# Opening of a two-layer decoder trunk: one modulation accumulator, scaling and rounding on ScalarE, products by parts

## The chip, the cores and the metric

The kernel runs on one core of a Trainium2 chip. The metric is the device time of one execution in microseconds (us). The engines of a core work side by side, each through its own list of instructions in order: TensorE (PE, matmuls; PEld is its weight load), VectorE (DVE), ScalarE (ACT), GpSimd (POOL) and SyncE (SP), which here starts the loads from memory. Times inside a profile are counted from the start of the profiled execution's span.

## The reference

Two layers, each of a SwiGLU half step, a token mixer and another SwiGLU half step. Every sub-layer normalizes its input and modulates it with shift and scale, which come from the condition c through mod_w:

```python
c_act = jax.nn.silu(c)
for i in range(DEPTH):
    mod = (c_act @ mod_w[i] + mod_b[i]).reshape(B, N_SUBLAYERS, 3, D)
    shift, scale, gate = mod[:, :, 0], mod[:, :, 1], mod[:, :, 2]
    h = modulate(rms_norm(x, norm_g[i, 0]), shift[:, 0], scale[:, 0])
    x = x + MACARON_WEIGHT * gate[:, 0, None, :] * swiglu(h, ffn_w_gate[i, 0], ffn_w_up[i, 0], ffn_w_down[i, 0])
    ...
```

with modulate(h, shift, scale) = h * (1 + scale) + shift and swiglu(h) = (silu(h @ w_gate) * (h @ w_up)) @ w_down. x has 256 tokens of 1024 channels, the SwiGLU has 2816 inner columns, all in float32. The change lies in the first sub-layer of the first layer: its rms_norm, its shift and scale, and the first 1536 columns of h @ w_gate and h @ w_up.

## The kernel before

A float32 product is made of three faster ones. Each operand is split into a rounded high part and the low rest: ScalarE copies the raw tile into the high part (wh, hTh), VectorE subtracts that from the raw values (wl, hTl), and TensorE adds wh x hTh, wh x hTl and wl x hTh in one PSUM bank (mm_blocks, L389 to L391). A matmul there takes 128 weight columns and 256 tokens.

open_trunk (L671 to L845) is the opening. VectorE, ScalarE, GpSimd, TensorE and SP run it in the order in which the code issues it. It first loads c and x, gets the row statistics (square on ScalarE, rms_scale on VectorE and GpSimd), scales x by them (u, L708, VectorE), transposes it on TensorE and copies it to xT (L712, ScalarE). Shift and scale of the 1024 channels are not ready then. They are made in four groups of two k-tiles (a k-tile is 128 channels): reduce multiplies eight 128-row slices of mod_w (tiles oraw, 128x512) with c and adds them up on VectorE (L756 opens an accumulator, L758 adds to it) into two accumulators, cacc0 and cacc1; modulate sums these over the partitions with products against a column of ones on TensorE (L770), makes scale and shift columns of the result (sb, three short VectorE steps), then h from xT (hk, L780, VectorE), its high part (hTh, L783, ScalarE) and its low part (hTl, L786, VectorE).

With a group's two k-tiles of h, TensorE can do six pieces of 12 matmuls: for each k-tile the first 512 gate columns, the first 512 up columns, and the next 512 gate columns. A group needs three weight tiles (raw, 128x1024): (0,k) holds gate and up columns of one k-tile, (1,k) the next gate columns of both. split makes wh on ScalarE (L743) and wl on VectorE (L744). There are four raw buffers and eight for pairs of oraw slices.

The table OPEN_HOLD sets how many pieces of a group are held back behind the next group's column sum (3, 2, 2), OPEN_SPLIT how many weight tiles are split ahead of the sb steps (2, 2, 2, 1), OPEN_HEAD and OPEN_MEAN where the next group's accumulations stand. After the last group the general weight stream starts (Weights, L215 for its wl, L206 for its wh), with up columns of the same SwiGLU. The two casts idr<-ident (L1026) belong to tables for the later attention and only stand in VectorE's list here; they wait for a memset of idr on GpSimd (L1024).

## Time and profile before

| | us |
|---|---|
| median of 3 runs | 1229.28 |
| lowest, highest run | 1228.28, 1230.29 |
| profiled execution, its own time | 1230.24 |
| its span, first to last instruction | 1228.5 |
| TensorE busy | 1202.4 |
| VectorE busy | 936.6 |
| ScalarE busy | 657.4 |

The profile is one execution. Busy time of TensorE counts the time in which a matmul is under way. A share over the whole span says little of the opening, the first 62 us of it; that stretch is read from its own rows.

### The profile page before, as it was taken

The numbers are of one execution on the slowest core, as the hardware profiler recorded it, in microseconds if no ns is written. First come the engines' busy times: TensorE is split into PE (matmuls) and PEld (weight loads), VectorE is DVE, ScalarE is ACT, GpSimd is POOL, SyncE is SP. The second block draws the span as 40 slices with busy tenths as digits, with TensorE's granted clock in tenths as the row PEclk, the third lists the DMA queues.
The fourth block names the chain that finished last, engine by engine and source line by source line (L and its number), as shares of the span: only waits on it lengthen the run. The fifth ranks groups of instructions, "written<-read, shape, count | busy, mean of one in ns | idle before, by whom it ended". The sixth has DMA issues, their size and how long they took to land.

```text
span 1228.5 us, 21017 instructions
## 1 busy us (share of the span) xinstructions
PE 1202.4 (98%) x8130; PEld 1085.5 (88%) x8130; DVE 936.6 (76%) x1318; ACT 657.4 (54%) x1002; POOL 101.9 (8%) x130
## 2 busy tenths in 40 slices
PE   6999999999999999999999999999999999999998
PEld 5999988878779999889999887888888787999987
DVE  7878777998788887579978659978686877765653
ACT  4446444676654554444554435677575665544540
POOL 1000000222100000000000003131131200000000
PEclk9999999999999999999999999999999999999999
DMA  9879885695739988638888647656545552866461
GB/s 334 277 269 327 304 317 182 199 306 201 272 99 341 330 275 310 206 111 292 305 277 325 206 154 235 210 181 211 175 154 182 197 173 86 289 203 217 168 213 42
DMA packets 152069, 281.21 MB, mean 229 GB/s; under 512 B 13424, under 2 KB 79504, under 8 KB 151968
## 3 DMA queue, kind: packets, MB, share of 16 engines
q1 hardware_dynamic: 151968, 279.85, 68.4%
q8 instruction: 64, 1.05, 0.3%
q14 instruction: 37, 0.30, 0.1%
HBM read 277.71 MB, written 2.10 MB: 228 GB/s over the span
## 4 chain that ended last, share of the span: by engine, by line
PE 76%; DVE 9%; DMA 5%; issue 4%; POOL 2%; ACT 2%; SPq 0%; POOLq 0%; DVEq 0%; ACTq 0%
PE block_bank L389 13%; PE block_bank L391 13%; PE block_bank L390 13%; PE bank L394 11%; PE bank L395 11%; PE bank L396 11%; DMA mraw<-in_mod_w_dram 3%; DVE wl L215 2%; POOL hrs L860 2%; DVE acc L296 1%; DVE lo L924 1%; PE obank L949 1%; DMA raw<-in_dil_w_in_dram 1%; DMA raw<-in_fox_w_in_dram 1%; ACT wh L206 1%
## 5 line engine op out<-in xcount | busy, mean ns | idle before, releaser
L215 DVE TENSOR_TENSOR wl<-raw,wh 128x1024 fp32r<-128x1024 f32 (+1 forms) x360 | 434.9, 1216 | 160.1 <-ACT wh L206 156.8
L206 ACT CAST wh<-raw 128x1024 fp32r<-128x1024 f32 (+1 forms) x360 | 374.5, 1046 | 299.2 <-PE bank L396 107.2
L389 PE MATMUL block_bank<-hTh,wh 128*128 128x256 f32 x1312 | 371.6, 283 | 2.0 <-ACT hTh L783 2.0
L391 PE MATMUL block_bank<-hTh,wl 128*128 128x256 f32 x1312 | 371.4, 283 | 0.0
L390 PE MATMUL block_bank<-hTl,wh 128*128 128x256 f32 x1312 | 370.7, 283 | 0.0
L389 PEld LDWEIGHTS block_bank<-hTh,wh 128*128 128x128 f32 x1312 | 248.5, 189 | 2.5 <-ACT hTh L783 2.1
L390 PEld LDWEIGHTS block_bank<-hTl,wh 128*128 128x128 f32 x1312 | 248.2, 189 | 0.5 <-DVE hTl L786 0.2
L391 PEld LDWEIGHTS block_bank<-hTh,wl 128*128 128x128 f32 x1312 | 248.0, 189 | 0.0
L394 PE MATMUL bank<-wh,hTh 128*128 128x512 f32 (+2 forms) x496 | 192.0, 387 | 0.8 <-DVE nm L924 0.8
L396 PE MATMUL bank<-wh,hTl 128*128 128x512 f32 (+2 forms) x496 | 181.6, 366 | 0.0
L395 PE MATMUL bank<-wl,hTh 128*128 128x512 f32 (+2 forms) x496 | 181.0, 365 | 0.0
L296 DVE SCALAR_TENSOR_TENSOR acc<-mraw,ccols,acc 128x1024 f32<-128x1024 f32 x112 | 143.4, 1281 | 29.8 <-DMA mraw<-in_mod_w_dram 29.3
L395 PE MATMUL bank<-wl,aTh 128*128 128x512 f32 (+1 forms) x420 | 146.4, 349 | 0.0
L394 PE MATMUL bank<-wh,aTh 128*128 128x512 f32 (+1 forms) x420 | 146.1, 348 | 0.0
L396 PE MATMUL bank<-wh,aTl 128*128 128x512 f32 (+1 forms) x420 | 145.7, 347 | 0.0
L396 PEld LDWEIGHTS bank<-wh,hTl 128*128 128x128 f32 x496 | 93.2, 188 | 16.5 <-DVE hTl L471 0.5
L394 PEld LDWEIGHTS bank<-wh,hTh 128*128 128x128 f32 x496 | 93.6, 189 | 14.0 <-DVE nm L924 1.2
L395 PEld LDWEIGHTS bank<-wl,hTh 128*128 128x128 f32 x496 | 93.7, 189 | 12.3
L394 PEld LDWEIGHTS bank<-wh,aTh 128*128 128x128 f32 x420 | 79.5, 189 | 10.8
L396 PEld LDWEIGHTS bank<-wh,aTl 128*128 128x128 f32 x420 | 79.3, 189 | 10.5
L395 PEld LDWEIGHTS bank<-wl,aTh 128*128 128x128 f32 x420 | 79.5, 189 | 10.1
L926 ACT ACTIVATE lo<-lo,nm 128x128 f32<-128x128 f32 (+1 forms) x64 | 37.8, 591 | 64.8 <-DVE nm L924 64.7
(225 smaller groups left out, 1280.9 us busy)
## 6 DMA issues: line engine op xcount, KB each, us to landing
mraw<-in_mod_w_dram SPq DMA_DIRECT2D x128, 512.0 KB, 5.2
raw<-in_ffn_w_down_dram SPq DMA_DIRECT2D x88, 512.0 KB, 4.1
raw<-in_ffn_w_gate_dram SPq DMA_DIRECT2D x76, 512.0 KB, 4.4
raw<-in_ffn_w_up_dram SPq DMA_DIRECT2D x76, 512.0 KB, 4.6
raw<-in_dil_w_in_dram SPq DMA_DIRECT2D x128, 256.0 KB, 4.2
raw<-in_fox_w_in_dram SPq DMA_DIRECT2D x36, 256.0 KB, 4.8
oraw<-in_mod_w_dram SPq DMA_DIRECT2D x32, 256.0 KB, 6.3
raw<-in_ffn_w_gate_dram SPq DMA_DIRECT2D x24, 256.0 KB, 6.0
```

The costliest lines, as they stand in the source:

```text
L206: act.copy(wh, self.raws[self.hi])
L215: dve.tensor_sub(wl, self.raws[self.lo], wh.bitcast(F32))
L296: dve.scalar_tensor_tensor(acc, raw, ccol[:, k:k + 1], self.bias_tile if k == 0 else acc, op0=OP.mult, op1=OP.add)
L389: pe.matmul(out_i, wh[:, blk], hTh[:, :, k, :], start=first and i % 2 == 0, stop=False)
L390: pe.matmul(out_i, wh[:, blk], hTl[:, :, k, :], start=False, stop=False)
L391: pe.matmul(out_i, wl[:, blk], hTh[:, :, k, :], start=False, stop=last and i % 2 == 1)
L394: pe.matmul(o, ah, wh, start=first, stop=False)
L395: pe.matmul(o, ah, wl, start=False, stop=False)
L396: pe.matmul(o, al, wh, start=False, stop=last)
L860: nc.gpsimd.tensor_tensor(rs, ms, mhalf, op=OP.pow)
L924: dve.tensor_tensor_reduce(out=lo[:, 0:n], in0=lg[:, 0:n], in1=m, scale=-1.0, scalar=BIG, op0=OP.add, op1=OP.min, accum_out=nm)
L926: act.activation(lo[:, 0:n], lo[:, 0:n], AF.Exp, bias=nm, scale=-1.0, accum_out=sums[:, t, i:i + 1])
```

## The change

Each group has one accumulator, opened by VectorE in group 0 and by ScalarE in the others, so its column sum has half as many products. Scaling of x moves to ScalarE, all accumulations of group 0 stand after it, and the columns of norm_g and mod_b are transposed between the two token tiles. hTh is made by ScalarE straight from xT, with scale and bias as per-partition operands; hk by VectorE in group 0 and by ScalarE afterwards. split is parted into split_hi and split_lo. The products of a piece run by parts (mm_parts): four with wh and hTh, four with wh and hTl, four with wl and hTh. One piece is held back in each group. Loads are issued in the same order.

```diff
-OPEN_HEAD = 4
-OPEN_SPLIT = (2, 2, 2, 1)
-OPEN_MEAN = (1, 2, 2)
-OPEN_HOLD = (3, 2, 2)
+OPEN_HOLD = 1
...
+    def mm_parts(o, k, wh, wl, first, last):
+
+        for w, h in ((wh, hTh), (wh, hTl), (wl, hTh)):
+            for i in range(4):
+                blk = slice(i * P, (i + 1) * P)
+                pe.matmul(o[i // 2][:, i % 2], w[:, blk], h[:, :, k, :], start=first and w is wh and h is hTh and
+                          i % 2 == 0, stop=last and w is wl and i % 2 == 1)
...
-        def normalize(t):
-            ss = main.tile([P, 2], F32, tag="ss", bufs=4, name="ss")
-            for h in range(2):
-                square(t, h, slice(h * 512, (h + 1) * 512), ss)
-            rs = rms_scale(ss)
...
-            def half(h):
-                xn = main.tile([P, 512], F32, tag="u", bufs=3, name="u")
-                dve.tensor_scalar(xn, x[t][:, h * 512:(h + 1) * 512], rs, None, op0=OP.mult)
-                tp = bank4()
-                for k in range(4):
-                    pe.transpose(tp[:, k, :], xn[:, k * P:(k + 1) * P], ident)
-                act.copy(xT[:, t, h * 4:(h + 1) * 4, :], tp)
-
-            return [lambda: half(0), lambda: half(1)]
+        def normalize():
+
...
+            held = []
+            for t in range(NT):
+                for h in range(2):
+                    xn = main.tile([P, 512], F32, tag="u", bufs=3, name="u")
+                    act.activation(xn, x[t][:, h * 512:(h + 1) * 512], AF.Copy, scale=rs[t])
+                    tp = bank4()
+                    for k in range(4):
+                        pe.transpose(tp[:, k, :], xn[:, k * P:(k + 1) * P], ident)
+                    held.append((xT[:, t, h * 4:(h + 1) * 4, :], tp))
+                    if len(held) == 3:
+                        act.copy(*held.pop(0))
+                if t == 0:
+                    columns(gb8, 3, gbcol)
+            for dst, tp in held:
+                act.copy(dst, tp)
...
-        def split(key):
+        def split_hi(key):
             raw = ws[key]
             wh = wp.tile([P, 2, 512], F32R, tag="wh", name="wh")
             wl = wp.tile([P, 2, 512], F32R, tag="wl", name="wl")
             act.copy(wh, raw)
-            dve.tensor_sub(wl, raw, wh.bitcast(F32))
-            ws[key] = wh, wl
+            ws[key] = wh, wl, raw
             uses[key] = 2
             weights.live += 1
 
+        def split_lo(key):
+            wh, wl, raw = ws[key]
+            dve.tensor_sub(wl, raw, wh.bitcast(F32))
+
...
-        def reduce(q, rows, extra=()):
+        def reduce(q, k):
             n = groups[q][1]
-            for k in rows:
-                if k < 2:
-                    accs[q, k] = pool.tile([P, 2, 2 * P], F32, tag=f"cacc{k}", bufs=2, name=f"cacc{k}")[:, :, 0:n * P]
-                    dve.tensor_scalar(accs[q, k], raws[q, k], ccol[:, k:k + 1], None, op0=OP.mult)
+            if k == 0:
+                accs[q] = pool.tile([P, 2, 2 * P], F32, tag="cacc", bufs=2, name="cacc")[:, :, 0:n * P]
+                if q:
+                    act.activation(accs[q], raws[q, k], AF.Copy, scale=ccol[:, k:k + 1])
                 else:
-                    dve.scalar_tensor_tensor(accs[q, k % 2], raws[q, k], ccol[:, k:k + 1], accs[q, k % 2],
-                                                   op0=OP.mult, op1=OP.add)
-                if extra:
-                    extra.pop(0)()
-
-        def modulate(q, between, meanwhile):
+                    dve.tensor_scalar(accs[q], raws[q, k], ccol[:, k:k + 1], None, op0=OP.mult)
+            else:
+                dve.scalar_tensor_tensor(accs[q], raws[q, k], ccol[:, k:k + 1], accs[q], op0=OP.mult, op1=OP.add)
+
+        def modulate(q):
+
             k0, n = groups[q]
             cp = bank()
-            terms = [(accs[q, i], ones.bitcast(F32)[:, 0:1]) for i in range(2)]
             for j in range(2):
                 for i in range(n):
-                    for m, (a, c) in enumerate(terms):
-                        pe.matmul(cp[:, n * j + i:n * j + i + 1], a[:, j, i * P:(i + 1) * P], c,
-                                         start=m == 0, stop=m == len(terms) - 1)
-            between()
+                    pe.matmul(cp[:, n * j + i:n * j + i + 1], accs[q][:, j, i * P:(i + 1) * P],
+                              ones.bitcast(F32)[:, 0:1], start=True, stop=True)
...
-            hk = pool.tile([P, NT, 2, P], F32, tag="hk", bufs=2, name="hk")
+            hk = pool.tile([P, 2, NT, P], F32, tag="hk", bufs=2, name="hk")
             for i in range(n):
-                dve.tensor_scalar(hk[:, :, i, :], xT[:, :, k0 + i], sb[:, 1, i:i + 1], sb[:, 0, i:i + 1],
-                                        op0=OP.mult, op1=OP.add)
-            for t in range(NT):
-                act.copy(hTh[:, t, ks, :], hk[:, t, 0:n])
-            meanwhile()
-            for t in range(NT):
-                dve.tensor_sub(hTl[:, t, ks, :], hk[:, t, 0:n], hTh[:, t, ks, :].bitcast(F32))
+                act.activation(hTh[:, :, k0 + i, :], xT[:, :, k0 + i], AF.Identity, scale=sb[:, 1, i:i + 1],
+                               bias=sb[:, 0, i:i + 1])
+                if q:
+                    act.activation(hk[:, i], xT[:, :, k0 + i], AF.Identity, scale=sb[:, 1, i:i + 1],
+                                   bias=sb[:, 0, i:i + 1])
+                else:
+                    dve.tensor_scalar(hk[:, i], xT[:, :, k0 + i], sb[:, 1, i:i + 1], sb[:, 0, i:i + 1],
+                                      op0=OP.mult, op1=OP.add)
+                yield lambda i=i: dve.tensor_sub(hTl[:, :, k0 + i, :], hk[:, i], hTh[:, :, k0 + i, :].bitcast(F32))
...
             k = wk + (i if w else 0)
-            mm_blocks(outs[o], k, wh[:, i], wl[:, i], k == 0, k == KT - 1)
+            mm_parts(outs[o], k, wh[:, i], wl[:, i], k == 0, k == KT - 1)
             uses[w, wk] -= 1
...
         load_mod(0, range(KT))
         load_weights(0)
-        halves = normalize(0) + normalize(1)
-        reduce(0, range(KT), halves)
-        columns(gb8, 3, gbcol)
+        normalize()
+        for k in range(KT):
+            reduce(0, k)
         backlog = []
         for q in range(nq):
-            todo = keys(q)
+            units, more = keys(q), range(0)
             if q:
                 load_weights(q)
-                reduce(q, rest)
-
-            def between():
-                for _ in range(OPEN_SPLIT[q]):
-                    if todo:
-                        split(todo.pop(0))
-
-            def meanwhile():
-                if q + 1 < nq:
-                    load_mod(q + 1, range(KT))
-                    reduce(q + 1, range(OPEN_MEAN[q]))
-
-            modulate(q, between, meanwhile)
-            while todo:
-                split(todo.pop(0))
+            split_hi(units[0])
+            lows = modulate(q)
+            next(lows)()
+            split_lo(units[0])
+            for low in lows:
+                low()
+            for u in units[1:]:
+                split_hi(u)
             if q + 1 < nq:
-                reduce(q + 1, range(OPEN_MEAN[q], OPEN_HEAD))
-            else:
+                load_mod(q + 1, range(KT))
+                reduce(q + 1, 0)
+                more = range(1, KT)
+            early = 2 if q else 0
+            for i, u in enumerate(units[1:]):
+                for k in more[early * i:early * (i + 1)]:
+                    reduce(q + 1, k)
+                split_lo(u)
+            for k in more[early * (len(units) - 1):]:
+                reduce(q + 1, k)
+            if q + 1 == nq:
                 weights.start()
             for piece in backlog:
                 products(piece)
             todo = pieces(q)
-            cut = len(todo) if q == nq - 1 else max(0, len(todo) - OPEN_HOLD[q])
+            cut = len(todo) if q == nq - 1 else len(todo) - OPEN_HOLD
             for piece in todo[:cut]:
                 products(piece)
```

**Place 1, VectorE, group 0's accumulations.** In the listings, msq and u are statistics and scaled x, cacc0, cacc1 and cacc the accumulators, oraw slices of mod_w. Before:

```order
L407 SCALAR_TENSOR_TENSOR msq_149<-ss_144 128x1
L756 TENSOR_SCALAR cacc0_153<-oraw_115,ccols_87 128x512
L708 TENSOR_SCALAR u_155<-x0_83,rs_142 128x512
L756 TENSOR_SCALAR cacc1_163<-oraw_115,ccols_87 128x512
L708 TENSOR_SCALAR u_165<-x0_83,rs_142 128x512
L758 SCALAR_TENSOR_TENSOR cacc0_153<-oraw_118,ccols_87,cacc0_153 128x512
```

VectorE at the same place in the change:

```order
L412 SCALAR_TENSOR_TENSOR msq_149<-ss_144 128x1
L1042 CAST idr_965<-ident_74 16x16 x2
L693 COPY gbcol_88<-bank_167 128x24
L774 TENSOR_SCALAR cacc_188<-oraw_115,ccols_87 128x512
L776 SCALAR_TENSOR_TENSOR cacc_188<-oraw_115,ccols_87,cacc_188 128x512
L776 SCALAR_TENSOR_TENSOR cacc_188<-oraw_118,ccols_87,cacc_188 128x512 x2
```

The scaling of x has gone, and the idr casts and the gbcol copy, which stood behind the eight accumulations, stand ahead of the first.

**Place 2, VectorE and ScalarE between the column sums of groups 1 and 2.** wl_341 is the low part of the tile of group 1's second k-tile before, wl_338 the same in the change; wl_452 and wl_456 are tiles of group 2, wl_315 and wl_335 tiles (0,2) and (1,2) of group 1; the accumulations are group 2's. VectorE before, from the end of hk on:

```order
L756 TENSOR_SCALAR cacc0_334<-oraw_322,ccols_87 128x512
L756 TENSOR_SCALAR cacc1_336<-oraw_322,ccols_87 128x512
L786 TENSOR_TENSOR hTl_86<-hk_317,hTh_85 128x256 x2
L744 TENSOR_TENSOR wl_341<-raw_289,wh_340 128x1024
L758 SCALAR_TENSOR_TENSOR cacc0_334<-oraw_325,ccols_87,cacc0_334 128x512
L758 SCALAR_TENSOR_TENSOR cacc1_336<-oraw_325,ccols_87,cacc1_336 128x512
L758 SCALAR_TENSOR_TENSOR cacc0_334<-oraw_328,ccols_87,cacc0_334 128x512
L758 SCALAR_TENSOR_TENSOR cacc1_336<-oraw_328,ccols_87,cacc1_336 128x512
L758 SCALAR_TENSOR_TENSOR cacc0_334<-oraw_331,ccols_87,cacc0_334 128x512
L758 SCALAR_TENSOR_TENSOR cacc1_336<-oraw_331,ccols_87,cacc1_336 128x512
L744 TENSOR_TENSOR wl_452<-raw_430,wh_451 128x1024
L744 TENSOR_TENSOR wl_456<-raw_433,wh_455 128x1024
```

VectorE in the change, from the end of the sb steps on:

```order
L801 TENSOR_TENSOR hTl_86<-hk_326,hTh_85 128x2x128
L763 TENSOR_TENSOR wl_315<-raw_306,wh_314 128x1024
L801 TENSOR_TENSOR hTl_86<-hk_326,hTh_85 128x2x128
L776 SCALAR_TENSOR_TENSOR cacc_352<-oraw_340,ccols_87,cacc_352 128x512
L776 SCALAR_TENSOR_TENSOR cacc_352<-oraw_343,ccols_87,cacc_352 128x512
L763 TENSOR_TENSOR wl_335<-raw_309,wh_334 128x1024
L776 SCALAR_TENSOR_TENSOR cacc_352<-oraw_343,ccols_87,cacc_352 128x512
L776 SCALAR_TENSOR_TENSOR cacc_352<-oraw_346,ccols_87,cacc_352 128x512
L763 TENSOR_TENSOR wl_338<-raw_311,wh_337 128x1024
L776 SCALAR_TENSOR_TENSOR cacc_352<-oraw_346,ccols_87,cacc_352 128x512
L776 SCALAR_TENSOR_TENSOR cacc_352<-oraw_349,ccols_87,cacc_352 128x512 x2
```

ScalarE at this place before, from the last split ahead of the column sum to the first of the next group:

```order
L743 CAST wh_309<-raw_287 128x1024
L783 CAST hTh_85<-hk_317 128x256 x2
L743 CAST wh_340<-raw_289 128x1024
L743 CAST wh_451<-raw_430 128x1024
L743 CAST wh_455<-raw_433 128x1024
```

ScalarE in the change, over the same stretch:

```order
L793 ACTIVATE hTh_85<-xT_108,sb_322 128x2x128
L796 ACTIVATE hk_326<-xT_108,sb_322 128x256
L793 ACTIVATE hTh_85<-xT_108,sb_322 128x2x128
L796 ACTIVATE hk_326<-xT_108,sb_322 128x256
L756 CAST wh_334<-raw_309 128x1024
L756 CAST wh_337<-raw_311 128x1024
L772 ACTIVATE cacc_352<-oraw_340,ccols_87 128x512
```

The low part of the second k-tile's tile stood right behind hTl and ahead of six accumulations; now four accumulations and another tile's low part stand ahead of it, and the first of these accumulations reads what ScalarE writes last in its listing.

**Place 3, TensorE, from the second to the third piece of group 1.** Before, in pieces of the same weight tiles:

```order
L389 MATMUL block_bank_112<-hTh_85,wh_305 128x256
L390 MATMUL block_bank_112<-hTl_86,wh_305 128x256
L391 MATMUL block_bank_112<-hTh_85,wl_306 128x256
L389 MATMUL block_bank_109<-hTh_85,wh_340 128x256
L390 MATMUL block_bank_109<-hTl_86,wh_340 128x256
L391 MATMUL block_bank_109<-hTh_85,wl_341 128x256
```

TensorE in the change:

```order
L395 MATMUL block_bank_112<-hTh_85,wl_315 128x256 x2
L395 MATMUL block_bank_109<-hTh_85,wh_337 128x256 x2
L395 MATMUL block_bank_110<-hTh_85,wh_337 128x256 x2
L395 MATMUL block_bank_109<-hTl_86,wh_337 128x256 x2
L395 MATMUL block_bank_110<-hTl_86,wh_337 128x256 x2
L395 MATMUL block_bank_109<-hTh_85,wl_338 128x256 x2
L395 MATMUL block_bank_110<-hTh_85,wl_338 128x256 x2
```

The products with the low part wl_338 now come ninth to twelfth in the piece; before, the first of them was the third product.

## Rows read from the trace of the kernel before

**Rows 1.** The page: busy us, share of the span, instructions, by engine.

```profile
PE 1202.4 (98%) x8130; PEld 1085.5 (88%) x8130; DVE 936.6 (76%) x1318; ACT 657.4 (54%) x1002; POOL 101.9 (8%) x130
```

**Rows 2.** Busy time by stretch; after the colon its length, then each engine.

```profile
core 0: us, PE busy (x) PEld busy (x) DVE busy (x) ACT busy (x) POOL busy (x), PEclk, DMA share, GB/s
...
19.85:61.80 41.95, 41.95 (x338) 41.75 (x339) 37.12 (x63) 18.78 (x25) 0.00 (x0) 1.00 0.89 299
61.80:230.00 168.20, 168.19 (x1182) 157.07 (x1181) 134.89 (x142) 84.52 (x105) 5.47 (x9) 1.00 0.78 266
```

**Rows 3.** TensorE in order of time: start, duration, engine, line, operation, tiles.

```profile
19.85 0.58 PE L389 MATMUL block_bank<-hTh,wh 128*128 128x256 f32 x1 [2.03 <-ACT hTh L783]
...
24.35 0.33 PE L390 MATMUL block_bank<-hTl,wh 128*128 128x256 f32 x1
...
26.41 1.84 PE L770 MATMUL bank<-ones,cacc 128*128 128x1 f32 x16
28.11 0.36 PE L389 MATMUL block_bank<-hTh,wh 128*128 128x256 f32 x1
...
38.15 1.84 PE L770 MATMUL bank<-ones,cacc 128*128 128x1 f32 x16
...
48.47 1.84 PE L770 MATMUL bank<-ones,cacc 128*128 128x1 f32 x16
...
61.54 0.28 PE L391 MATMUL block_bank<-hTh,wl 128*128 128x256 f32 x1
```

**Rows 4.** VectorE in order of time, in the opening.

```profile
7.68 0.49 DVE L756 TENSOR_SCALAR cacc<-oraw,ccols 128x512 f32<-128x512 f32 x1
...
11.89 2.73 DVE L758 SCALAR_TENSOR_TENSOR cacc<-oraw,ccols,cacc 128x512 f32<-128x512 f32 x4
...
14.63 0.33 DVE L1026 CAST idr<-ident 16x16 fp32r<-16x16 f32 x2
...
17.86 0.16 DVE L775 SCALAR_TENSOR_TENSOR sb<-bank,gbcol 128x2 f32<-128x2 f32 x1 [0.32 <-PE bank L770]
...
18.32 0.73 DVE L780 TENSOR_SCALAR hk<-xT,sb 128x256 f32<-128x256 f32 x2
...
36.61 2.35 DVE L744 TENSOR_TENSOR wl<-raw,wh 128x1024 fp32r<-128x1024 f32 x2
```

**Rows 5.** GpSimd in order of time, the memset of idr.

```profile
10.58 0.38 POOL L1024 MEMSET idr<- 128x16 f32 x1
```

**Rows 6.** VectorE in order of time after the opening, a single accumulator.

```profile
71.37 1.28 DVE L296 SCALAR_TENSOR_TENSOR acc<-mraw,ccols,bias 128x1024 f32<-128x1024 f32 x1
72.68 1.28 DVE L296 SCALAR_TENSOR_TENSOR acc<-mraw,ccols,acc 128x1024 f32<-128x1024 f32 x1
```

**Rows 7.** VectorE by line, 0 to 62 us: busy us, mean ns, idle before.

```profile
L758 DVE SCALAR_TENSOR_TENSOR cacc<-oraw,ccols,cacc 128x512 f32<-128x512 f32 x24 | 16.5, 749 | 0.0
L786 DVE TENSOR_TENSOR hTl<-hk,hTh 128x256 fp32r<-128x256 f32 x8 | 3.0, 420 | 0.6 <-ACT hTh L783 0.5
```

**Rows 8.** ScalarE by line, whole span; nm in L926 is a per-partition operand.

```profile
L926 ACT ACTIVATE lo<-lo,nm 128x512 f32<-128x512 f32 x32 | 23.2, 724 | 42.9 <-DVE nm L924 42.9
...
L926 ACT ACTIVATE lo<-lo,nm 128x256 f32<-128x256 f32 x16 | 8.2, 513 | 9.1 <-DVE nm L924 9.0
...
L783 ACT CAST hTh<-hk 128x256 fp32r<-128x256 f32 x8 | 2.9, 405 | 15.6 <-DVE hk L780 15.6
```

**Rows 9.** ScalarE in order of time, two casts of weight tiles.

```profile
52.20 2.00 ACT L743 CAST wh<-raw 128x1024 fp32r<-128x1024 f32 x2
```

**Rows 10.** TensorE in order of time: its longest wait at the higher clock.

```profile
1021.67 0.88 PE L949 MATMUL obank<-pt,v 128*64 128x128 f32 x12 [1.74 <-DVE on L966]
```

**Rows 11.** Busy time by stretch, around that wait.

```profile
1019.00:1023.00 4.00, 2.26 (x34) 1.97 (x32) 3.01 (x4) 2.66 (x6) 0.00 (x0) 1.00 0.45 148
```

**Rows 12.** SP's queue in order of time, the fifth weight load.

```profile
18.93 0.38 SPq L736 DMA_DIRECT2D raw<-in_ffn_w_gate_dram  x1
```

**Rows 13.** The loads of tile oraw, 0 to 62 us, issue to landing.

```profile
DMA to landing us min/median/max: 4.1/6.3/6.8
```

More of the change, by code (lines that the diff above doesn't have):

```diff
@@ L698, in open_trunk @@
         uses = {}
-        def normalize(t):
-            ss = main.tile([P, 2], F32, tag="ss", bufs=4, name="ss")
-            for h in range(2):
-                square(t, h, slice(h * 512, (h + 1) * 512), ss)
-            rs = rms_scale(ss)
-            def half(h):
-                xn = main.tile([P, 512], F32, tag="u", bufs=3, name="u")
-                dve.tensor_scalar(xn, x[t][:, h * 512:(h + 1) * 512], rs, None, op0=OP.mult)
-                tp = bank4()
-                for k in range(4):
-                    pe.transpose(tp[:, k, :], xn[:, k * P:(k + 1) * P], ident)
-                act.copy(xT[:, t, h * 4:(h + 1) * 4, :], tp)
-            return [lambda: half(0), lambda: half(1)]
+        def normalize():
+            rs = []
+            for t in range(NT):
+                ss = main.tile([P, 2], F32, tag="ss", bufs=4, name="ss")
+                for h in range(2):
+                    square(t, h, slice(h * 512, (h + 1) * 512), ss)
+                rs.append(rms_scale(ss))
+            held = []
+            for t in range(NT):
+                for h in range(2):
+                    xn = main.tile([P, 512], F32, tag="u", bufs=3, name="u")
[10 more added lines that the diff above has]
+                act.copy(dst, tp)
         def load_mod(q, rows):
@@ L794, in products @@
             w, wk, i, o = piece
[L795 removed]
+            wh, wl, _ = ws[w, wk]
             k = wk + (i if w else 0)
[L797 removed]
+            mm_parts(outs[o], k, wh[:, i], wl[:, i], k == 0, k == KT - 1)
             uses[w, wk] -= 1
```

2 lines of the change are left out of this document (removed).

## The prediction

> **What bounds the kernel now.** I read the page's shares first, then stretches by engine, then the opening in order of time on TensorE, VectorE, GpSimd and ScalarE. TensorE is busy 98% of the span [rows 1]. From 19.85 us to 61.8 it is busy for 41.95 of 41.95 us and then for 168.19 of 168.20 [rows 2]: once its first product has started, nothing makes it wait, and the opening's four groups run on it back to back. So the change is worth three things: when the first product starts, how much work TensorE gets, and what it has to wait for that it did not wait for before. A shift at the end of the opening stays to the end, since the next 168 us have no idle time to take it up, and code and loads behind it are the same.
>
> [Rows 3] give the units. The 16 column-sum products of a group (L770) take 28.11 - 26.41 = 1.70 us; 84 products take 38.15 - 28.11 = 10.04, 0.1195 each, so a piece of 12 takes 1.43; a whole group period (72 products and one column sum) is 48.47 - 38.15 = 10.32. Products are 0.21 us apart up to 24.35 and 0.12 after, at 256 columns the lower and the higher of TensorE's two clocks (the PEclk column reads 1.00 for both [rows 2]); the lower one held for 4.5 us from the first product, 21 products. The 288th and last product of the opening starts at 61.54.
>
> **The change part by part.** I set a zero at the end of each group's column sum and walk the queues as the listings in the section on the change have them; on VectorE and ScalarE each instruction waits for the one ahead.
>
> *Column sums.* One accumulator needs half the products: 8, 0.85 us, of which 0.14 more is the last one's tail. In groups 1 to 3 this lies on TensorE's path: 0.85 less each.
>
> *The start.* Before, VectorE's eight accumulations for group 0 run from 7.68 to 14.62 [rows 4], interleaved with the scaling of x. Now the scaling is gone from VectorE, but the two idr casts stand ahead of the first accumulation, and they wait for GpSimd's idr memset, which ends at 10.96 [rows 5]. Before, these casts ran at 14.63, behind everything that counted. With about 0.27 for the casts and the 24-column copy (0.33 for two casts in [rows 4], less their overlap) the first accumulation starts at 11.23, 3.55 later. The chain is also slower per link. On one accumulator each step waits for the end of the one before: two such steps start 1.31 apart at 1.28 each [rows 6], so 0.03 is added to the 0.749 of an accumulation [rows 7], 0.78 a step; on two alternating accumulators four take 2.73, 0.66 a step [rows 4]. 11.23 + 0.52 + 7 x 0.78, less the last 0.03, is 17.18, against 14.62. Then the column sum: before, 15 of the 16 products take 14.62 to 17.86 [rows 4], 0.216 each; now 8, 1.78 with the wait: 18.96. The three sb steps, 0.46 [rows 4], end at 19.42. Before came two hk (0.73) and two hTh; now one hTh on ScalarE. Its price is not in the trace: 128x256 from SBUF takes 0.405 as a cast and 0.513 with one per-partition operand [rows 8]; this one has two, scale and bias. I take 0.513 + 0.108 = 0.62, since that is the nearest row plus its own step; the ends are 0.405 (operands free) and 0.724 (the row of twice the columns). First product at 20.1, against 19.85: 0.25 later, the shorter column sum and the shorter chain to h nearly paying for the later accumulations.
>
> *Group 0.* Five pieces are issued now instead of three before the next column sum. With the lower clock as long as before, 60 products end at 20.1 + 4.5 + 39 x 0.1195 = 29.3. VectorE: hTl 20.5, wl 21.7, hk and hTl 22.4, two wl (2.35 [rows 4]) 24.75, seven accumulations 30.2. The column sum starts at 30.2 and ends at 31.2. Before, 60 products and this sum were done at 28.11 + 24 x 0.1195 = 30.98: 0.2 behind.
>
> *Groups 1 and 2, the main term.* Zero is the end of the group's column sum. sb is ready at 0.49. ScalarE: hTh, hk, hTh, hk, 0.52 apart, to 2.6; two casts, 0.95 apart (2.00 for two [rows 9]), to 4.55; the scaling that opens the next group's accumulator, 0.72 (the 128x512 row with one such operand [rows 8]), to 5.25. VectorE: hTl of the first k-tile at 2.1 (its hk ends at 1.67), wl of the first tile at 3.3, hTl of the second k-tile at 3.65. Then it stands before an accumulation that waits for ScalarE's 5.25. Two accumulations to 6.83, wl of the tile that TensorE needs last to 7.96, two accumulations to 9.45, wl of the second k-tile's tile at 10.7. TensorE: the held piece to 1.43, the first parts of piece 1 with a wait of 0.2 for hTl, its wl part with a wait of 0.7 at 3.34, piece 2 to 5.25, two parts of piece 3 to 6.2. Its third part needs that last wl: 10.75, a wait of 4.55. The other 28 products to 14.1, the column sum to 15.1 (the accumulations are done at 13.0). Before the period was 10.32, and VectorE split two of the three tiles ahead of sb and kept the accumulations behind the third one. 15.1 - 10.32 = 4.78, twice: 9.55.
>
> *Group 3* has no accumulations behind it: the last wl is ready at 6.0, before TensorE wants it at 6.2. The waits of 0.2 and 0.7 stay: 0.9.
>
> *Covered.* Scaling x on ScalarE is four steps of about 0.72; with the four copies to xT that is under 6 us of ScalarE from 7.7 on, when the statistics are there [rows 4], so xT is done by 14, 5 us before its first use at 19.4. The same number of products by parts costs TensorE nothing else. SP's fifth weight load waits for the first tile's wl, issued at 18.93 before [rows 12]; that wl is now done at 21.7, the next such one at 23.6, and behind these loads queue the next group's mod_w loads, all on SP's one queue. From 23.7 with 6.3 us to land [rows 13] and 0.88 apart (my estimate: 256 KB at the stretch's 299 GB/s [rows 2]) the first of them is there by 31 and the last by 37; the first is wanted at 31.2 + 4.5 = 35.7 and the last at 42: hidden by over 4 us. Without that cover each us late would be one on the sum.
>
> The sum is 0.2 + 9.55 + 0.9 = 10.65 us, 1240.9 against the profiled execution's 1230.24 (span 1228.5 and 1.74 around it). The median of the runs is 0.96 lower, so **1240.0**. With the ScalarE operands free each group's chain is 0.95 shorter: 8.3, 1237.6. With the upper price, 11.9, 1241.2.
>
> The Trainium skill, "ScalarE: Activation LUTs", section What ACT_TABLE_LOAD costs, gives 186 ns plus 0.833 ns an element and 93 ns for each per-partition operand. By that the step would be 0.585 (an estimate from that page), and the sum 10.3; the trace's 0.513 for one operand agrees with its 0.49.
>
> **The rivals.** *The clock falls in the waits.* TensorE stands still for 4.55 us twice. In the trace of before its longest wait after the clock rose is 1.74 us, and the stretch around it keeps 1.00 [rows 10, 11]; no row shows what 4.5 us do. If the lower clock returns for as long as at the start, 21 products cost 0.094 more each, 2.0 us a time: 1242 for one wait, 1244 for both. The Trainium skill, "TensorE: Matmul & The Clock Gate", section Why this matters for your kernels, warns that idle gaps between bursts of matmuls bring the half clock back; by that rule it would be 1244, and the row of 1.74 us neither supports nor refutes it.
>
> *ScalarE is cheaper than I take it,* or the accumulator step follows closer: 1236.5 to 1238.
>
> *VectorE keeps up (the other side).* If the last wl were there when TensorE reaches the third piece, only the shorter column sums would be left, 3 x 0.85 less: 1226.7. The place is the third piece of groups 1 and 2; the point from which it decides is 6.2 us after the column sum, against 10.7 by the queue. Four accumulations (3.0) and the wait for ScalarE (1.6) would both have to vanish. For it speaks that VectorE has less to do in all; against it that its queue is in order and that the four accumulations stand ahead of that wl.
>
> **How the numbers follow.** The forecast 0.63 (its own range 1238.5 to 1241.5), the falling clock 0.22, cheaper ScalarE 0.10, VectorE keeping up 0.05. The range 1236 to 1245 takes in the first three with the ends of the ScalarE price, and a later or earlier rise of the clock at the start (1 us either way). About 0.2%, 2.5 us, is what a measurement of this kernel tells from no change. Slower 0.94, within 0.02, faster 0.04.
>
> **What would show it.** In the changed kernel's profile: the first accumulation at about 11.2 behind idr; the first product near 20.1; on TensorE two waits of about 4.5 us on VectorE's wl, 6 us after the column sums of groups 1 and 2, 15 us apart; no such wait in group 3; the opening's last product near 72. The forecast is wrong if the wl row comes ahead of the accumulations in time, if these waits are under 2 us, if the opening's end shifts by another amount than the total, or if products after the waits are 0.21 apart, which is the first rival.

## The result and the profile after

The changed kernel takes 1244.66 us (median of 4 runs, 1239.55 to 1248.14) against 1229.7 for the kernel before (median of 4): a ratio of 1.0119, 95% interval [1.0096, 1.0142], or 15.0 us. In a second comparison it took 1245.84 us (1.0116, [1.0099, 1.0133]). It is slower, as forecast, and the time lies within the range. But it is 4.7 us over the 1240.0 of the likeliest case, above that case's own range, and next to the 1244 of a rival, the falling clock.

The first profiled execution (1242.86 us, span 1241.1) stands 12.6 us over that of before. Its two stretches, columns as in [rows 2]:

```profile
19.54:74.31 54.77, 44.30 (x312) 42.49 (x312) 36.63 (x54) 22.85 (x32) 0.00 (x0) 0.94 0.67 219
74.31:243.00 168.69, 168.68 (x1185) 157.58 (x1184) 137.21 (x145) 87.13 (x109) 5.47 (x9) 1.00 0.79 270
```

In [rows 2] the opening was 41.95 us with TensorE busy for all of it. Now it is 54.77, 44.30 of them busy, at a mean granted clock of 0.94; behind it TensorE is again busy without a break. All of the loss lies in the opening. TensorE there, in order of time (answers to [rows 3]):

```profile
19.54 1.23 PE L395 MATMUL block_bank<-hTh,wh 128*128 128x256 f32 x4 [1.21 <-ACT hTh L793]
...
29.74 1.02 PE L784 MATMUL bank<-ones,cacc 128*128 128x1 f32 x8 [0.77 <-DVE cacc L776]
30.62 0.72 PE L395 MATMUL block_bank<-hTh,wh 128*128 128x256 f32 x4
...
34.01 0.74 PE L395 MATMUL block_bank<-hTh,wl 128*128 128x256 f32 x4 [0.39 <-DVE wl L763]
...
36.49 0.63 PE L395 MATMUL block_bank<-hTl,wh 128*128 128x256 f32 x4
41.20 1.22 PE L395 MATMUL block_bank<-hTh,wl 128*128 128x256 f32 x4 [4.08 <-DVE wl L763]
42.22 1.05 PE L395 MATMUL block_bank<-hTh,wh 128*128 128x256 f32 x4
...
44.73 0.64 PE L395 MATMUL block_bank<-hTh,wh 128*128 128x256 f32 x4
...
46.96 0.73 PE L395 MATMUL block_bank<-hTh,wh 128*128 128x256 f32 x4
...
57.60 0.74 PE L395 MATMUL block_bank<-hTh,wl 128*128 128x256 f32 x4 [4.09 <-DVE wl L763]
...
63.35 0.72 PE L395 MATMUL block_bank<-hTh,wh 128*128 128x256 f32 x4
...
74.43 0.28 PE L386 MATMUL block_bank<-hTh,wh 128*128 128x256 f32 x1
```

The two long waits stand where the prediction put them, on a wl of VectorE in the third piece of groups 1 and 2. A group period is 46.96 - 30.62 = 16.34, then 16.39, against 10.32. Four products take 1.05 us behind a wait and 0.64 from 44.73 on. VectorE between the two column sums, in order of time:

```profile
32.39 0.43 DVE L801 TENSOR_TENSOR hTl<-hk,hTh 128x256 fp32r<-128x256 f32 x1 [1.17 <-ACT hk L796]
32.73 1.22 DVE L763 TENSOR_TENSOR wl<-raw,wh 128x1024 fp32r<-128x1024 f32 x1
33.87 0.42 DVE L801 TENSOR_TENSOR hTl<-hk,hTh 128x256 fp32r<-128x256 f32 x1
35.89 1.54 DVE L776 SCALAR_TENSOR_TENSOR cacc<-oraw,ccols,cacc 128x512 f32<-128x512 f32 x2 [1.60 <-ACT cacc L772]
37.34 1.22 DVE L763 TENSOR_TENSOR wl<-raw,wh 128x1024 fp32r<-128x1024 f32 x1
38.48 1.53 DVE L776 SCALAR_TENSOR_TENSOR cacc<-oraw,ccols,cacc 128x512 f32<-128x512 f32 x2
39.93 1.22 DVE L763 TENSOR_TENSOR wl<-raw,wh 128x1024 fp32r<-128x1024 f32 x1
41.06 2.32 DVE L776 SCALAR_TENSOR_TENSOR cacc<-oraw,ccols,cacc 128x512 f32<-128x512 f32 x3
```

The wl that starts at 39.93 is the one for which TensorE stands still until 41.20. Ahead of it are two pairs of accumulations (1.5 us each), the other tile's wl, and 1.60 us of waiting for ScalarE's opening step. The granted clock behind the wait (stretch, length, busy times, then the clock in the third column from the end):

```profile
36.40:41.20 4.80, 0.72 (x7) 0.51 (x6) 4.73 (x7) 0.39 (x1) 0.00 (x0) 1.00 0.42 141
41.20:44.65 3.45, 3.45 (x16) 3.45 (x17) 2.11 (x3) 0.00 (x0) 0.00 (x0) 0.51 0.96 305
44.65:46.00 1.35, 1.35 (x13) 1.35 (x13) 0.00 (x0) 0.00 (x0) 0.00 (x0) 1.00 0.99 337
```

TensorE stands still at the higher of its two levels (2.4 GHz), and as the products resume the granted clock is 0.51, the lower level (1.2 GHz), for about 3.4 us. The same follows the second wait, 0.7 us after the products resume (0.50 from 58.30 to 61.72).

### The profile page after: what moved, and what is told of

It is laid out like the page before. It is cut to its first block, busy times and chain, and to the rows that moved or that the text cites. A ratio compares the mean times of both kernels' runs of the same rounds, so it can differ in the third digit from the quotient of the medians.

```text
span 1241.1 us, 20959 instructions
## 1 busy us (share of the span) xinstructions
PE 1202.1 (97%) x8098; PEld 1085.2 (87%) x8098; DVE 933.8 (75%) x1305; ACT 665.8 (54%) x1015; POOL 99.9 (8%) x130
## 3 DMA queue, kind: packets, MB, share of 16 engines
q8 instruction: 63, 1.03, 0.3%
## 4 chain that ended last, share of the span: by engine, by line
PE 69%; DVE 11%; DMA 7%; issue 5%; ACT 4%; POOL 3%; SPq 1%; POOLq 0%; DVEq 0%; ACTq 0%
PE block_bank L388 12%; PE block_bank L387 12%; PE block_bank L386 12%; PE bank L399 10%; PE bank L400 10%; PE bank L401 10%; DMA mraw<-in_mod_w_dram 4%; DVE wl L212 3%; POOL hrs L876 2%; DVE acc L293 1%; PE block_bank L395 1%; DVE lo L940 1%; ACT wh L203 1%; DVE hms L873 1%; DMA oraw<-in_mod_w_dram 1%
## 5 line engine op out<-in xcount | busy, mean ns | idle before, releaser
L388 PE MATMUL block_bank<-hTh,wl 128*128 128x256 f32 x1216 | 343.6, 283 | 0.0
L386 PE MATMUL block_bank<-hTh,wh 128*128 128x256 f32 x1216 | 343.3, 282 | 0.0
L387 PE MATMUL block_bank<-hTl,wh 128*128 128x256 f32 x1216 | 342.7, 282 | 0.0
L386 PEld LDWEIGHTS block_bank<-hTh,wh 128*128 128x128 f32 x1216 | 229.5, 189 | 0.4
L387 PEld LDWEIGHTS block_bank<-hTl,wh 128*128 128x128 f32 x1216 | 229.2, 188 | 0.3
L388 PEld LDWEIGHTS block_bank<-hTh,wl 128*128 128x128 f32 x1216 | 229.0, 188 | 0.0
L399 PEld LDWEIGHTS bank<-wh,hTh 128*128 128x128 f32 x496 | 93.6, 189 | 13.9 <-DVE nm L940 1.1
L400 PEld LDWEIGHTS bank<-wl,aTh 128*128 128x128 f32 x420 | 79.5, 189 | 10.1
```

Source lines behind the costliest of these rows:

```text
L386: pe.matmul(out_i, wh[:, blk], hTh[:, :, k, :], start=first and i % 2 == 0, stop=False)
L387: pe.matmul(out_i, wh[:, blk], hTl[:, :, k, :], start=False, stop=False)
L388: pe.matmul(out_i, wl[:, blk], hTh[:, :, k, :], start=False, stop=last and i % 2 == 1)
L399: pe.matmul(o, ah, wh, start=first, stop=False)
L400: pe.matmul(o, ah, wl, start=False, stop=False)
```

## The experiments

The theory: on VectorE the accumulations of the next group stand ahead of the last wl, and no low part of a group's tiles is made ahead of its sb any more; so TensorE waits, and in the waits loses its clock. Rivals: the parts of the change cost the time by themselves (the single accumulator's chain, ScalarE's way to h, products by parts), or ScalarE's late opening step alone does.

**All low parts first.**

```
-            early = 2 if q else 0
+            early = 0
```

> The changed kernel with one number different: VectorE makes all low parts wl of a group ahead of the next group's accumulations (early = 0). Main theory (the accumulations that stand ahead of the last wl on VectorE make TensorE wait): the two waits of 4.1 us for wl vanish. In their place the column sums of groups 2 and 3 wait about 2 us for the accumulations, which then run from about 6 to 11.4 us after the column sum ahead of them; the period of groups 1 and 2 is about 12.3 instead of 16.3, TensorE's clock stays up throughout, and the time is some 8 us under the changed kernel, near 1236, still 5 to 6 us over the kernel before. Rival (the longer way to h through ScalarE, or the products by parts, make the wait): the 4 us waits stay and the time stays within 2 us of the changed kernel's.

Measured: 1237.33 us, 1.0053 [1.0033, 1.0072], 6.8 over before. TensorE:

```profile
34.15 0.73 PE L395 MATMUL block_bank<-hTh,wl 128*128 128x256 f32 x4 [0.39 <-DVE wl L763]
...
42.35 1.02 PE L784 MATMUL bank<-ones,cacc 128*128 128x1 f32 x8 [1.77 <-DVE cacc L776]
...
54.88 1.44 PE L784 MATMUL bank<-ones,cacc 128*128 128x1 f32 x8 [1.77 <-DVE cacc L776]
```

The waits of 4 us are gone, and the column sums wait 1.77 us for the accumulations, as expected. The clock was a miss: it stayed up through the first wait of 1.77, but from 54.88 to 62.30 it is 0.54. VectorE, from one sb to the next:

```profile
30.95 0.16 DVE L788 SCALAR_TENSOR_TENSOR sb<-bank,gbcol 128x2 f32<-128x2 f32 x1 [1.21 <-PE bank L784]
...
32.53 0.43 DVE L801 TENSOR_TENSOR hTl<-hk,hTh 128x256 fp32r<-128x256 f32 x1 [1.16 <-ACT hk L796]
...
36.73 5.47 DVE L776 SCALAR_TENSOR_TENSOR cacc<-oraw,ccols,cacc 128x512 f32<-128x512 f32 x7
43.41 0.16 DVE L788 SCALAR_TENSOR_TENSOR sb<-bank,gbcol 128x2 f32<-128x2 f32 x1 [1.21 <-PE bank L784]
```

Of 12.46 us VectorE waits 1.16 for ScalarE's hk and 1.21 for the column sum, and works the rest, 10.1. So VectorE now bounds the period: before, it filled such waits with the next group's wl, the two at 36.61 in [rows 4].

**The accumulator opened on VectorE.**

```
-                if q:
-                    act.activation(accs[q], raws[q, k], AF.Copy, scale=ccol[:, k:k + 1])
-                else:
-                    dve.tensor_scalar(accs[q], raws[q, k], ...)
+                dve.tensor_scalar(accs[q], raws[q, k], ...)
```

> The changed kernel, but every group's accumulator is opened by VectorE, as before, so VectorE no longer waits for ScalarE there. Main theory (VectorE's queue sets the wait; its wait of 1.6 us for ScalarE's opening step is part of it): the last wl comes 0.7 to 1.1 us earlier and TensorE's two waits shrink from 4.1 to 3.0 to 3.4 us; if the clock still falls in them the time is about 2 us under the changed kernel, if not about 5. Rival (ScalarE's late opening step is the whole of it): the waits vanish, and the time is 12 us lower, at the kernel before.

Measured: 1242.07 us, 1.0089 [1.0072, 1.0106], 11.5 over before. TensorE's two waits:

```profile
40.51 0.74 PE L395 MATMUL block_bank<-hTh,wl 128*128 128x256 f32 x4 [2.42 <-DVE wl L763]
...
55.73 1.22 PE L395 MATMUL block_bank<-hTh,wl 128*128 128x256 f32 x4 [2.92 <-DVE wl L763]
```

The last wl starts 39.23 - 31.10 = 8.13 us after the first product behind the column sum, against 39.93 - 30.62 = 9.31: 1.2 us earlier, slightly more than expected. TensorE's waits are 2.42 and 2.92 us, not 0, so ScalarE's opening is a part of the wait and not the whole. The second shrinks by just these 1.2 us. The first shrinks by 0.5 more because TensorE comes to it later, at the lower clock (0.53 from 31.00 to 34.60). The clock falls three times in this opening.

**The wanted tile second.**

```
             units, more = keys(q), range(0)
+            units = [units[0], units[2], units[1]]
```

> The changed kernel, but the tile that TensorE needs for its third piece, that of the group's second k-tile, is split second instead of third, so two accumulations instead of four stand ahead of its wl. Main theory: the wait at the third piece shrinks from 4.1 to 1.0 to 1.8 us, each accumulation ahead of it being worth 0.78 us and the tile between 1.15. As the accumulations still end about 12.5 to 13 us after the column sum, the next column sum now waits for them, the period is 13 to 14 us, the clock does not fall, and the time is 5 to 7 us under the changed kernel. Rival (accumulations have nothing to do with it): no change.

Measured: 1238.89 us, 1.0068 [1.0053, 1.0083], 8.3 over before. TensorE's first wait for wl, and the one of its next column sum:

```profile
38.57 0.74 PE L395 MATMUL block_bank<-hTh,wl 128*128 128x256 f32 x4 [1.49 <-DVE wl L763]
...
43.48 1.02 PE L784 MATMUL bank<-ones,cacc 128*128 128x1 f32 x8 [1.33 <-DVE cacc L776]
```

TensorE's waits for wl are 1.49 and 1.02, and its column sums wait 1.33 and 1.32 us for the accumulations; the periods are 13.8 and 13.9. Two accumulations and a tile fewer ahead of the wl took 2.6 us off the first wait, as expected: the order sets it. Of the 3.1 off the second, 0.5 is TensorE coming later, at the lower clock. The clock falls behind both of the column sums' waits (0.54 from 44.60 to 48.20), which had not been expected.

**TensorE kept busy in the waits.** In the third piece of groups 1 and 2, fill is 30. The output is not used; the products are extra work.

```
         for w, h in ((wh, hTh), (wh, hTl), (wl, hTh)):
+            if fill and w is wl:
+                spare = block_bank()
+                for i in range(fill):
+                    pe.matmul(spare[:, i % 2], wh[:, 0:P], hTh[:, :, k, :], start=i == 0, stop=i == fill - 1)
```

> The changed kernel with 30 extra products into a spare bank in front of the part that waits, in groups 1 and 2: about 3.6 us of work at the higher clock, inside the wait of 4.1 us. All else as in the changed kernel. If the clock falls because TensorE stands still in these waits, it now keeps the higher clock through both, the products behind the waits are 0.12 apart instead of 0.21, and the time is 3 to 3.5 us lower than the changed kernel's, with the waits themselves ending at the same distance from the column sum. If the clock falls for another reason (what follows the wait), it falls here too and the time is the same or higher.

Measured: 1242.2 us, 1.0092 [1.0077, 1.0107], 11.6 over before, against 15.0 and 15.5 for the change. TensorE, and its stretches around the first wait:

```profile
37.05 3.72 PE L397 MATMUL block_bank<-hTh,wh 128*128 128x256 f32 x30
41.29 0.75 PE L400 MATMUL block_bank<-hTh,wl 128*128 128x256 f32 x4 [0.52 <-DVE wl L768]
...
71.48 0.28 PE L387 MATMUL block_bank<-hTh,wh 128*128 128x256 f32 x1
```

```profile
36.40:41.20 4.80, 4.37 (x37) 4.16 (x36) 4.73 (x7) 1.05 (x1) 0.00 (x0) 1.00 0.44 148
41.20:44.65 3.45, 3.36 (x28) 3.36 (x29) 2.21 (x4) 0.00 (x0) 0.00 (x0) 1.00 1.01 316
```

The wl comes at the same time, the clock stays at 1.00, and 28 products run where 16 did. The next group starts 14.81 us after the last instead of 16.34, and then 14.88 instead of 16.39. So each fall cost 1.5 us in the first profile, and work that nobody needs made the opening 2.95 us shorter. (The intervals of the whole times overlap, from 1.0096 to 1.0107, so the evidence is the trace.) Of its 11.6 us, 9.8 are in the opening (the product behind its 288th starts at 71.48; before, the 288th at 61.54). Behind it this execution has one low stretch (0.50 from 334.8 on); whether such a stretch is the rest in the other runs isn't known.

**The parts alone, in the kernel before.** Four kernels, each with one part of the change. One accumulator, by the edit

```
-                if k < 2:
+                if k < 1:
...
-                    dve.scalar_tensor_tensor(accs[q, k % 2], raws[q, k], ccol[:, k:k + 1], accs[q, k % 2], ...)
+                    dve.scalar_tensor_tensor(accs[q, 0], raws[q, k], ccol[:, k:k + 1], accs[q, 0], ...)
...
-            terms = [(accs[q, i], ones.bitcast(F32)[:, 0:1]) for i in range(2)]
+            terms = [(accs[q, i], ones.bitcast(F32)[:, 0:1]) for i in range(1)]
```

> The kernel before with one part of the change alone: one accumulator per group instead of two, opened on VectorE, half the column-sum products. VectorE's order of wl and accumulations is that of before. If the change's cost is the order on VectorE and not the single accumulator, no wait of 4 us appears. The shorter column sums are worth up to 3 x 0.85 us; against that each of 7 steps of a group's chain takes 0.78 instead of 0.66, 0.8 us more of VectorE in a group, and VectorE has little idle time there. So within 0.2% of before: between 2.5 us faster and 1 us slower, likely 0 to 1 us slower. Rival (the chain on one accumulator is itself the cost): each of groups 1 to 3 starts over 1 us later, 3 us slower or more.

x scaled on ScalarE, ahead of group 0's accumulations in the code and no longer interleaved with them:

```
-                dve.tensor_scalar(xn, x[t][:, h * 512:(h + 1) * 512], rs, None, op0=OP.mult)
...
+                    act.activation(xn, x[t][:, h * 512:(h + 1) * 512], AF.Copy, scale=rs[t])
...
-        reduce(0, range(KT), halves)
+        reduce(0, range(KT))
```

> The kernel before with the scaling of x moved from VectorE to ScalarE, and nothing else. The accumulations of the first group are no longer interleaved with four scalings of about 0.3 us; but they also wait for the loads of mod_w, so the first product comes between 0 and 1.3 us earlier, and the time is within 0.2% of before. Rival (ScalarE is late with xT): the first product comes later than 19.9 and the time is 1 us or more longer.

Products by parts (mm_parts of the change in place of mm_blocks):

> The kernel before with the products of a k-tile issued by parts (hTh by wh for all four column blocks, then hTl by wh, then hTh by wl) instead of by blocks. TensorE does the same products, and VectorE's results are there in time before; the spacing of 0.119 us stays, and the time is that of before within 0.1%, opening's last product at 61.5. Rival (changing the output bank's half at each product costs time): the spacing grows, and with 288 products each 0.01 us is 2.9 us.

hTh from xT on ScalarE:

```
-                dve.tensor_scalar(hk[:, :, i, :], xT[:, :, k0 + i], sb[:, 1, i:i + 1], sb[:, 0, i:i + 1], ...)
-            for t in range(NT):
-                act.copy(hTh[:, t, ks, :], hk[:, t, 0:n])
+                act.activation(hTh[:, :, k0 + i, :], xT[:, :, k0 + i], AF.Identity, scale=..., bias=...)
+                dve.tensor_scalar(hk[:, i], xT[:, :, k0 + i], sb[:, 1, i:i + 1], sb[:, 0, i:i + 1], ...)
...
```

> The kernel before with one part of the change alone: hTh rounded by ScalarE straight from xT with the group's scale and shift, while VectorE makes hk beside it (in all groups) for hTl. The path from sb to the first product loses one step of about 0.4 us (hk on VectorE ahead of the copy on ScalarE), so the first product comes 0.3 to 0.9 us earlier than 19.85; group 1's column sum waits for VectorE and takes part of it back. Time 0.3 to 0.9 us under before, within 0.2%. Rival (ScalarE's step with two operands is slow and costs on the path): the first product at 20 or later and the time 0.5 to 1 us over before.

Measured, against 1230.39 us of before on that chip:

| part | us | ratio, interval | first product | 288th product |
|---|---|---|---|---|
| before | 1230.39 | | 19.85 | 61.54 |
| one accumulator | 1230.37 | 1.0003 [0.9993, 1.0013] | 19.66 | 61.53 |
| x on ScalarE | 1230.84 | 1.0003 [0.9994, 1.0013] | 19.98 | 61.60 |
| by parts | 1230.43 | 1.0000 [0.9991, 1.0008] | 19.64 | 61.70 |
| hTh on ScalarE | 1230.25 | 1.0002 [0.9991, 1.0013] | 18.94 | 61.04 |

None of them costs anything measurable, and none gains. With one accumulator the column sums are shorter, and group 1's period is 39.20 - 28.23 = 10.97 us against 39.86 - 28.11 = 11.75 (84 products). But the next, of 72, is 10.97 too, against 10.32: VectorE's longer chain makes TensorE wait, 0.72 us of it for hTl. With hTh on ScalarE the first product is 0.91 earlier, and 0.50 of that is left at the end of the opening. With x on ScalarE the first product is 0.13 later, where 0 to 1.3 earlier was expected: the idr casts move in between the accumulations and wait 1.14 us for GpSimd, which takes back what the scaling gave.

**All parts, in the order of before.** The four parts above together, with hk also on ScalarE and the accumulator opened there, but modulate, split and reduce called in the order of the kernel before.

> The kernel before with all parts of the change (one accumulator, opened by ScalarE; x scaled, hTh and hk made on ScalarE; products by parts) but in the order of before on VectorE: two of a group's three tiles are split ahead of sb, two or three pieces are held back, and all but one of the accumulations stand behind the third tile's wl. If the order on VectorE is what cost 12 us in the profile, most of it goes: no wait over 2 us on TensorE after the first product, the clock stays up, and the time is 0 to 4 us over before (what is left being VectorE's waits for ScalarE's hk and opening step, 1.2 and 1.6 us a group). If the parts themselves cost it, the time stays within 4 us of the changed kernel's, 10 us or more over before.

Measured: 1234.04 us, 1.0031 [1.0019, 1.0043], 3.4 over before; some 12 of the 15 us are gone. TensorE's longest wait behind its first product, VectorE, and TensorE's stretch behind that wait:

```profile
27.58 1.57 PE L787 MATMUL bank<-ones,cacc 128*128 128x1 f32 x8 [1.73 <-DVE cacc L775]
...
32.79 0.75 DVE L775 SCALAR_TENSOR_TENSOR cacc<-oraw,ccols,cacc 128x512 f32<-128x512 f32 x1 [2.75 <-ACT cacc L771]
33.46 0.75 DVE L807 TENSOR_TENSOR hTl<-hk,hTh 128x256 fp32r<-128x256 f32 x2
```

```profile
27.60:34.70 7.10, 7.10 (x34) 7.10 (x35) 4.31 (x9) 3.62 (x6) 0.00 (x0) 0.52 1.08 362
```

What is left is that wait, VectorE's wait for ScalarE's opening step (2.75 us, with hTl queued behind it) and the lower clock for some 7 us, which had been expected to stay up. At 1.00 such a stretch would have held nearly 60 products, not 34.

**The other side: accumulations first in the kernel before.**

```
-            while todo:
-                split(todo.pop(0))
             if q + 1 < nq:
                 reduce(q + 1, range(OPEN_MEAN[q], OPEN_HEAD))
-            else:
+            while todo:
+                split(todo.pop(0))
+            if q + 1 == nq:
```

with OPEN_HEAD 6 instead of 4.

> The other side: the kernel before with six of the next group's accumulations moved ahead of the third tile's wl on VectorE, in all groups, and nothing else. If accumulations ahead of the last wl are enough to make TensorE wait for 4 us, two or three such waits appear and the time is 8 us or more over before. If it also takes that the first tiles' low parts are made behind sb and not ahead of it, as in the changed kernel, TensorE has work of two finished tiles and two held pieces to hide the third wl: its wait is under 1 us, and the time is 0 to 1 us over before.

Measured: 1230.69 us, 1.0001 [0.9991, 1.0010]. TensorE's one wait for wl:

```profile
46.91 0.39 PE L391 MATMUL block_bank<-hTh,wl 128*128 128x256 f32 x1 [0.50 <-DVE wl L744]
```

So accumulations ahead of the last wl are not enough by themselves. In the change two more things differ: the first tiles' low parts, too, are made behind sb, and only one held piece is left to run meanwhile. No run parts these two, so how the 4 us divide between them is not shown.

**A candidate.** Before, with hTh and the scaling of x on ScalarE, the idr casts on GpSimd, and one tile split ahead of the first sb.

> A candidate to beat both: the kernel before with hTh rounded by ScalarE straight from xT (hk on VectorE), x scaled on ScalarE, the two idr casts on GpSimd instead of VectorE, and one tile instead of two split ahead of the first sb. The accumulations of the first group end about 13, and the first product comes 1 to 2.4 us before 19.85. The column sum of group 1 then waits for VectorE, so that the opening's last product comes only about 0.5 us earlier than 61.5. Time 0.3 to 1 us under before, within 0.2%; if the start alone set the time, 2 us under.

Measured: 1229.96 us, 0.9990 [0.9981, 0.9999]. The first product comes at 17.84, 2.0 earlier, and the 288th at 61.05, 0.5 earlier. It beats the change; before it beats by 0.1%, which the interval, up to 0.9999, hardly tells from nothing: the column sum of group 1 waits for VectorE, and most of an early start is lost there.

**The change once more.**

> The changed kernel once more, beside the kernel before on the same chip, for a second profile and more times. The first profile gives 12.8 us in the opening, of which 9.7 are work and waits that the kernel with extra products in the waits still has, and 3.0 the lower clock behind the two waits. If that is all, the median is 12.6 to 13 us over before. The first comparison's median was 15 over, so 2 us more would have to come from further falls of the clock at other places; then this profile shows low stretches beside the two behind the waits, each worth 1.5 us, and the times spread over 5 us or more.

Measured: 1245.84 us, 1.0116 [1.0099, 1.0133], runs from 1241.75 to 1247.36; the profiled one is 1247.32, 4.5 over the first. TensorE, then ScalarE and VectorE at the start, then TensorE's stretches:

```profile
21.05 1.22 PE L395 MATMUL block_bank<-hTh,wh 128*128 128x256 f32 x4 [1.21 <-ACT hTh L793]
...
42.71 1.22 PE L395 MATMUL block_bank<-hTh,wl 128*128 128x256 f32 x4 [4.09 <-DVE wl L763]
...
60.11 1.22 PE L395 MATMUL block_bank<-hTh,wl 128*128 128x256 f32 x4 [4.10 <-DVE wl L763]
```

```profile
7.46 0.63 ACT L406 ACTIVATE junk<-x 128x512 bf16<-128x512 f32 x1 [1.66 <-DMA x<-in_x_dram]
...
8.83 0.16 DVE L412 SCALAR_TENSOR_TENSOR msq<-ss 128x1 f32<-128x1 f32 x1 [2.83 <-ACT junk L406]
...
11.26 0.40 DVE L1042 CAST idr<-ident 16x16 fp32r<-16x16 f32 x2 [2.28 <-POOL idr L1040]
```

```profile
41.00:42.00 1.00, 0.00 (x0) 0.00 (x0) 1.00 (x2) 0.00 (x0) 0.00 (x0) 0.79 0.78 170
42.00:42.70 0.70, 0.00 (x0) 0.00 (x0) 0.70 (x2) 0.00 (x0) 0.00 (x0) 0.50 1.07 397
42.71:48.30 5.59, 5.59 (x26) 5.59 (x27) 2.11 (x3) 0.00 (x0) 0.00 (x0) 0.50 0.98 299
```

The waits are the same, to 0.02 us. What differs is the lower clock and the start. Here the clock falls while TensorE still stands (0.79 from 41.00 to 42.00, then 0.50) and stays low for some 5.7 us of products behind the first wait and 5.4 behind the second, where the first profile had 3.4; the periods are 17.3 instead of 16.4, which makes 1.9 us. At the start ScalarE waits 1.66 us for the load of x's second token tile, for which it did not wait in the first profile; msq comes 1.5 us later than the 7.30 there, idr with it, and every accumulation stands behind idr. No low stretches at other places were needed: the expectation placed the further 2 us wrongly. Behind the opening 1.1 us more went; where is open.

## Why the prediction was right, and where it was off

*What bounds the kernel* held: behind the opening TensorE works without a break, so that the shift at the end of the opening (12.8 us by the 288th product, 74.31 against 61.54) is the shift of the span (12.6).

*The main mechanism* held, point by point: wl behind four accumulations, the opening step of ScalarE in front, TensorE's third piece waiting 6 us behind the column sum, no such wait in group 3. Nor does VectorE wait for a load in the opening, as forecast. By the terms of the sum, in the first profile and in that of the kernel with extra products:

| term | forecast | measured | with TensorE kept busy |
|---|---|---|---|
| start and group 0 | +0.2 | -0.36 | -0.26 |
| group 1, period less 10.32 | 4.78 | 6.02 | 4.49 |
| group 2, the same | 4.78 | 6.07 | 4.56 |
| group 3 | +0.9 | +1.04 | +1.03 |
| sum | 10.65 | 12.77 | 9.82 |

*The wait* was mis-sized by half a microsecond, 4.08 for 4.55: TensorE reached the third part of the third piece at 6.5 and not 6.2 us (its small waits), and the wl was there at 10.58 and not 10.75. The column sum took 0.81 and not 1.0. So with the clock up each of the two periods is 0.2 to 0.3 shorter than forecast.

*ScalarE's step* with two per-partition operands took 0.59 us, 0.50 apart, within the bounds and next to the 0.62 taken. By the costs that the Trainium skill, "ScalarE: Activation LUTs", section What ACT_TABLE_LOAD costs, states, the step would take 0.585 us (an estimate from that page); the trace's 0.59 agrees.

*The start* was taken from one row, idr's memset ending at 10.96 [rows 5]. In the change it ends at 9.7 in one execution and 11.2 in the other, behind GpSimd's statistics of x. So the first accumulation came at 10.41 and 11.91 around the forecast 11.23, and the first product at 19.54 and 21.05 around 20.1. The value was fair; that it moves from run to run, with the load of x that ScalarE waits for, was not seen.

*The clock* is the step that failed. The likeliest case kept it up, on the strength of one wait of 1.74 us that left it at 1.00 [rows 10, 11], and gave its fall a chance of 0.22. It fell in or behind both long waits in both profiles. Its price was put at 2.0 a wait; it is 1.5 where 3.4 us of products run at the lower clock (the experiment with extra products), and 0.9 to 1.0 more in the second profile, whose period is 17.3. The rival's 1244 is what the median shows, partly by luck: the first profile has 12.8 us in the opening and the second 16.1, on either side of the rival's 14.65, and 1.5 us between them is the start. The Trainium skill, "TensorE: Matmul & The Clock Gate", section Why this matters for your kernels, warns of just this for idle gaps between bursts; the rows of 4.08 and 4.09 us agree.

*VectorE keeps up*, the rival of the other side, fell: even with all low parts ahead of the accumulations, its 10.1 us of work and 2.4 of waiting make a period of 12.46.

## What to carry to other kernels

Taking work off a busy engine gained nothing here, because what was left stood in a worse order in its queue: look for the last result that the bounding engine wants, and count what is ahead of it. Keep some finished work of the next step ahead of each serial chain, as the kernel before did with two tiles' low parts and two or three held pieces; the same parts in that order cost 3 us instead of 15. When a change makes a busy TensorE stand still for microseconds, price the clock behind the wait too, as the likeliest case and not as a rival.

## What the runs showed of the hardware

The clock's fall is not set by the length of one wait alone. With all low parts first, a wait of 1.77 us left it up and the next of the same length brought it down in the same opening. Waits of 1.33 and 1.32 us brought it down (the wanted tile second), and so did one of 1.13 (the accumulator opened on VectorE); one of 1.22 in the second profile of the change and one of 1.74 in the kernel before did not. What decides is open.

The lower level lasted about 3.4 or about 6.8 us, in the same kernel and with the same wait of 4.09 us. Where it lasted 6.8, in the second profile of the change, its first microsecond or more fell into the wait. Of the 4.5 us between the two profiles of the change this is 1.9, the start 1.5, and 1.1 is open; so it is a part of why the changed kernel's runs spread over 5.6 and 8.6 us and those of before over 2 to 5. Products into a spare bank kept the clock up at no cost to the path: the wl came at the same time.

The granted clock does not tell all. At the start of the opening of the change the products are 0.21 us apart while it reads 1.00 (19.54 to 24.10); with all parts in the order of before it reads 0.50 there (20.00 to 24.00), and they are 0.21 apart as well. What holds back the products of the start is not shown.
